# Residual boundaries of a two-block transformer kernel: running sums that end with the sixth tile of eight

## The chip, the cores and the metric

The kernel runs on one core of a Trainium2 chip. Its time is the device time of one launch in microseconds (us). Five engines take part: PE (TensorE, matmuls), DVE (VectorE), ACT (ScalarE), POOL (GpSimd) and SP (SyncE, which issues DMAs here). Each engine works through a queue of its own, in an order that is fixed when the kernel is built; an instruction whose input is not there yet holds up all that stand behind it in the same queue.

## What is computed

x is 256 tokens by 1024 features in fp32. Two layers of a first block (attention, pooling and gated linear attention, beside a second sequence of 256 context tokens that is carried through the first layer only) and then a second block with two residual steps are applied. Every residual step has the form that follows, and the next stage begins with another norm of the new x:

```python
x = x + gate * rmsnorm(out, post_g)                   # out = merged @ w_out, 1024 features
z = (rmsnorm(x, pre_g) * (1 + scale) + shift) @ w_in  # the next stage
```

with `rmsnorm(x, g) = x * rsqrt(mean(x*x) + eps) * g`, the mean taken over the 1024 features of a token.

## The kernel before

x stands in SBUF with the features on the partitions: 8 tiles of 128 features by 256 tokens. A mean over features is thus a sum over 8 tiles and 128 partitions. All matmuls of weights are done three times (`mm3`, L442): each fp32 operand is split into a high part and a low rest (weights by `split`: a ScalarE cast, L425, and a subtraction, L427, by VectorE or GpSimd; activations in `build_h`), and hi*hi, hi*lo and lo*hi are added up. An output tile of a 1024-to-1024 projection is so 24 matmuls of 128x256 (`pwo`); the last projection (`pdn`) has 66 for a tile.

A residual boundary is the stretch between such a projection and the next one. There are five: the context and x between the two layers ("ctx" and "x" below, about 580 to 646 us of the profiled execution), x before the mixer of the second block ("mpre", about 985 to 1020 us), x before its feed-forward part ("fpre", about 1300 to 1336 us), and the last one, which ends in the output ("final").

The kernel computes what the second norm needs without waiting for the new x. With o the gained output, the mean of (x + r\*o)^2 is the mean of x^2, plus r times twice the mean of x\*o, plus r^2 times the mean of o^2. So `collect` takes each of the 8 projection tiles as it comes: ScalarE squares it (L512) and applies the gain to get o (L519; for the last tile VectorE, L517), VectorE multiplies o with x (L523), ScalarE squares o (L524). That gives three terms of 128x256 a tile. Running sums add them up over the tiles: VectorE adds the squares, GpSimd the products and the squares of o (all three L529). When they are complete, TensorE sums them over the partitions with 128x1 matmuls (`token_sums`, L461, into `ps_sa`), two 128-token halves for a term; fp32 makes each of them two records of the trace. VectorE copies the result to `part` (L540, L542).

`boundary` then sums the last tile's terms over the partitions (into `ps_ss`), adds `part` (m, L552), lets GpSimd raise it to the power -1/2 (L488, "the first pow"), spreads r over the partitions by two TensorE transposes (`ps_rb`, L469), sums the other two terms, and makes the new mean A in a chain of five small VectorE instructions (L565 to L569). A second pow and a second pair of transposes follow. `enter` goes through the 8 tiles: `update_x` does x + r\*o, on GpSimd for tiles 0, 1, 3, 5, 7 (L654, L655) and on VectorE for 2, 4, 6 (L657, L658); at the ctx boundary it is GpSimd for 2, 4, 6. `build_h` makes the normed tile (VectorE, L638), its high part (ScalarE, L640 or L643) and its low rest (VectorE, L641 or L644), and the next projection's matmuls (`pen`, `z1_...`; in the trace also `z_misc`) take it.

Where the tile framework's scheduler puts an instruction is decided at build time; `issue_after` asks that GpSimd's updates stand behind the pow.

Of the kernel before, what the change touches and what calls it, by code (L numbers as in the profile page):

```python
# [359 lines left out]
class B:  # L360
# [143 lines left out]
    def collect(self, st, ps, gain, xs, nxt=True):  # L504

        nc, S = self.nc, self.S
        n = ps.shape[-1]
        k = len(st["out"])
        if k == 0:
            st["acc"] = [S.cols(n) for _ in range(3 if nxt else 1)]  # L510
        terms = [S.cols(n) if k else a for a in st["acc"]]
        nc.scalar.activation(terms[0].ap, ps, AF.Square)  # L512
        o_ = S.cols(n)
        for i in range(n // 256):
            c = slice(256 * i, 256 * i + 256)
            if k == 7:
                nc.vector.tensor_scalar(o_.ap[:, c], ps[:, c], gain(k, i), None, ALU.mult)  # L517
            else:
                nc.scalar.mul(o_.ap[:, c], ps[:, c], gain(k, i))  # L519
        if nxt:  # L520
            for i in range(n // 256):
                c = slice(256 * i, 256 * i + 256)
                nc.vector.tensor_mul(terms[1].ap[:, c], o_.ap[:, c], xs[i][k])  # L523
            nc.scalar.activation(terms[2].ap, o_.ap, AF.Square)  # L524
        if k == 7:
            st["last"] = terms
        elif k:
            for e, a, t in zip((nc.vector, nc.gpsimd, nc.gpsimd), st["acc"], terms):
                e.tensor_add(a.ap, a.ap, t.ap)  # L529
            S.drop(*terms)  # L530
        st["out"].append(o_)
        if k == 6:

            m = n // P
            acc = [a.ap for a in st["acc"]]
            p_ = self.pb.tile([P, 512], F32, tag="p", name="ps_sa")
            for i, (a, f) in enumerate(zip(acc, ("mean", "mean2", "mean"))):
                self.token_sums(p_, i * m, a, f=self.c(f))
            st["part"] = self.sm.tile([P, 16], F32, tag="part", name="part")
            nc.vector.tensor_scalar(st["part"][:, :m], p_[:, :m], EPS, None, ALU.add)  # L540
            if nxt:
                nc.vector.tensor_copy(st["part"][:, m:3 * m], p_[:, m:3 * m])  # L542
            S.drop(*st["acc"])

    def boundary(self, st, A, n, nxt=True):

        nc = self.nc
        last, part = [t.ap for t in st["last"]], st["part"]
        ps = self.pa.tile([P, 512], F32, tag="p", name="ps_ss")
        self.token_sums(ps, 0, last[0], f=self.c("mean"))  # L550
        m = self.sm.tile([P, 16], F32, tag="m", name="m")[:, :n]
        nc.vector.tensor_add(m, ps[:, :n], part[:, 0:n])  # L552
        r = self.rsqrt(m, n)
        pr = self.bcast(r, n, self.pa)
        if not nxt:
            self.S.drop(*st["last"])
            return pr, None, None
        ps = self.pb.tile([P, 512], F32, tag="p", name="ps_ss")
        self.token_sums(ps, 0, last[1], f=self.c("mean2"))
        self.token_sums(ps, n, last[2], f=self.c("mean"))  # L560
        self.S.drop(*st["last"])
        t = self.sm.tile([P, 16], F32, tag="bt", name="bt")[:, :n]
        s12 = self.sm.tile([P, 16], F32, tag="bs", name="bs")[:, :2 * n]
        new = self.sm.tile([P, 16], F32, tag="bA", name="bA")[:, :n]
        nc.vector.tensor_add(s12, ps[:, :2 * n], part[:, n:3 * n])  # L565
        nc.vector.tensor_mul(t, r, s12[:, n:2 * n])
        nc.vector.tensor_add(t, t, s12[:, :n])
        nc.vector.tensor_mul(t, t, r)
        nc.vector.tensor_add(new, A, t)  # L569
        pr2 = self.bcast(self.rsqrt(new, n), n, self.pb)  # L570
        return pr, pr2, new

# [75 lines left out]
def update_x(b, k, st, xs, s_, pr, rs, on_pool):  # L648

    nc = b.nc  # L650
    o_ = st["out"][k]
    if on_pool:
        with b.tc.issue_after(b.chain_end.ins):
            nc.gpsimd.tensor_mul(o_.ap, o_.ap, rs.ap)  # L654
            nc.gpsimd.tensor_add(xs[s_][k], xs[s_][k], o_.ap)  # L655
    else:
        nc.vector.tensor_mul(o_.ap, o_.ap, pr[:, 0:256])  # L657
        nc.vector.tensor_add(xs[s_][k], xs[s_][k], o_.ap)  # L658
    b.S.drop(o_)


def enter(b, st, xs, s_, A, h, gain, shift, pool):

    pr, pr2, new = b.boundary(st, A, 2)
    rs = b.S.cols(256)
    b.nc.scalar.copy(rs.ap, pr[:, 0:256])
    for k in range(8):
        update_x(b, k, st, xs, s_, pr, rs, k in pool)
        build_h(b, k, xs, (s_,), gain, shift, pr2, *h(k))
        if k == 7:  # L670
            b.S.drop(rs)
        yield new


def trunk(b, l, xs, st, A):

    nc, S = b.nc, b.S
    full = l == 0
    ALLC, XC = slice(0, 512), slice(256, 512)
# [4 lines left out]
    v = b.vec(f"l{l}")  # L684
# [14 lines left out]
    if st is None:  # L699
        load_x(b, xs)  # L700
        mod_chunk(b, l, 0, True, lambda: first_units((2, 3)))
        ps = b.pa.tile([P, 512], F32, tag="p", name="ps_ss")
        for s_ in range(2):
            acc, t = S.cols(256), S.cols(256)
# [6 lines left out]
        A = b.sm.tile([P, 16], F32, tag="bA", name="bA")[:, :4]  # L711
# [5 lines left out]
    gain_, shift_ = (lambda k, s_: G[:, k, s_:s_ + 1]), (lambda k, s_: shift[:, k, s_:s_ + 1])  # L717
    if st is None:
        h = []
        for k in range(8):  # L720
            if k in MOD_AT:
                mod_chunk(b, l, MOD_AT.index(k) + 1, True)
            h.append((S.get(F32R), S.get(F32R)))
            build_h(b, k, xs, (0, 1), gain_, shift_, pr2, *h[k])
            for w, ps in zip(ws, pss):
                b.mm3(ps, w, h[k:], ALLC, off=k * P, start=k == 0, stop=k == 7)
        S.put(*b.slot[0])
    else:
        h, st = st
        xpart = enter(b, st, xs, 1, A[:, 2:4], lambda k: [t[:, XC] for t in h[k]], gain_, shift_, (0, 1, 3, 5, 7))  # L730
        A = next(xpart)
        for w, ps in zip(ws, pss):
            b.mm3(ps[:, 0:256], w, h, slice(0, 256))
        for k in range(8):
            if k:
                next(xpart)
            for w, ps in zip(ws, pss):
                b.mm3(ps[:, XC], w, h[k:k + 1], XC, off=k * P, start=k == 0, stop=k == 7)
        for _ in xpart:
            pass  # L740
# [523 lines left out]
    for j in range(0, 8, 2):  # L1264
        u = b.unit(("wo", l, j))
        for i in range(2):
            w = b.split(u[:, i * 1024:(i + 1) * 1024], 1024)
            ps = b.pmm.tile([P, 512], F32, tag="p", name="pwo")
# [19 lines left out]
    for w in held:  # L1288
        next(ctx)
        ps = b.pmm.tile([P, 512], F32, tag="p", name="pwo")  # L1290
# [177 lines left out]
def second_block(b, xs, st, A):  # L1468
    nc = b.nc
# [3 lines left out]
    v = b.vec("b2")  # L1473

    def pairs(h):
        return [(a, c) for a, c, _ in h]

    def halves():
        r_ = S.get(F32R)
        return r_[:, 0:256], r_[:, 256:512], r_  # L1480

    def column(w, name):
        ps = b.pmm.tile([P, 512], F32, tag="p", name=name)
        b.mm3(ps[:, C], w, hp, C)
        return ps
# [7 lines left out]
    def enter2(st, g, keys):  # L1493

        h, ws, pss = [], [], []
        for key in keys:
            u = b.unit(key)
            for i in range(2):
                if len(ws) < 3:
                    ws.append(b.split(u[:, i * 1024:(i + 1) * 1024], 1024))  # L1500
                    pss.append(b.pmm.tile([P, 512], F32, tag="p", name="pen"))

        def tile_(k):
            h.append(halves())
            return h[k][0:2]

        for k, new in enumerate(enter(b, st, xs, 1, A, tile_, lambda k, s_: v(g, k), None, (0, 1, 3, 5, 7))):
            for w, ps in zip(ws, pss):
                b.mm3(ps[:, C], w, pairs(h[k:]), C, off=k * P, start=k == 0, stop=k == 7)
        return h, new, pss, u[:, 1024:2048]  # L1510

    h, A, pss, rest = enter2(st, "mpre", [("win2", 14, 15), ("win2", 16, 17)])
    hp = pairs(h)
    cslots = b.unit_slots(("c2",), 3)
# [113 lines left out]
    for ps in (*pss, column(b.split(rest, 1024), "y")):  # L1628
        t = S.cols(256)
# [369 lines left out]
    st = {"out": []}  # L1999
    for j in range(0, 8, 2):  # L2000
        u = b.unit(("wo2", j))
        for i in range(2):
            w = b.split(u[:, i * 1024:(i + 1) * 1024], 1024)
            ps = b.pmm.tile([P, 512], F32, tag="p", name="pwo2")
# [3 lines left out]


    h, A, pss, rest = enter2(st, "fpre", [("up", 0), ("up", 1)])  # L2010
    hp = pairs(h)
    f = []
    nf = FF // P
    for j in range(nf):
# [3 lines left out]
        for i in range(2):  # L2018
            if j < 2 and 2 * j + i < 3:
                ps = pss[2 * j + i]  # L2020
            else:
                ps = column(b.split(rest if j == 1 else u[:, i * 1024:(i + 1) * 1024], 1024), "pup")
# [14 lines left out]
    st = {"out": []}  # L2037
    n = 0
    ps = None
    for un in range(11):  # L2040
        u = b.unit(("down", un))
        for i in range(2):
            hi, lo = b.split(u[:, i * 1024:(i + 1) * 1024], 1024)
            for k8 in range(8):
                k = n % nf
                if k == 0:
                    ps = b.pmm.tile([P, 512], F32, tag="p", name="pdn")
# [5 lines left out]
    pr, _, _ = b.boundary(st, A, 2, nxt=False)  # L2053
    rs = S.cols(256)
    nc.scalar.copy(rs.ap, pr[:, C])
    for k in range(8):
        o_ = st["out"][k]
# [63 lines left out]
```

## Time and profile before

| what | value |
|---|---|
| median of 3 runs | 1535.64 us (1535.45 to 1537.04) |
| the profiled execution's own time | 1536.71 us |
| its span, first to last instruction | 1534.9 us |
| mean granted TensorE clock | 0.96 |
| PE / PEld / DVE / ACT / POOL busy | 93% / 79% / 70% / 46% / 28% |

Rows below give the start (us), the length (us), the engine, the source line, the operation, the tiles, the shapes and, in brackets, the idle time of the engine just before and what ended it. The trace joins like instructions that follow one another: "x4" is four of them. The clock column is a share of TensorE's full 2.4 GHz; 0.5 is its lower level of 1.2 GHz.

### The profile page before, as it was taken

Reading aid. Unit: us, or ns where it says so; the run is one execution under the profiler, and the core shown is the slowest. Engines: PE = TensorE matmul, PEld = TensorE weight load, DVE = VectorE, ACT = ScalarE, POOL = GpSimd, SP = SyncE. Lnnn points to the kernel's source line nnn. Section 1 sums busy time; section 2 is a strip of 40 time slices with the busy share of each in tenths; the row PEclk is TensorE's granted clock in tenths of the full one; section 3 lists DMA queues with packets and bytes.
Section 4 is the critical chain, followed back from the end, with each engine's and each line's share of the span. In section 5 each row is a group of like instructions: output and inputs, shape, how many; then the busy total and the mean of one; then the engine's idle time right before and its main releaser. Section 6 shows DMA issues by size and latency. Waiting matters only on the chain. (4 is left out here: it accounts for less than half of the span.)

```text
span 1534.9 us, 27423 instructions
## 1 busy us (share of the span) xinstructions
PE 1427.4 (93%) x10700; PEld 1212.0 (79%) x10700; DVE 1070.7 (70%) x2113; ACT 713.5 (46%) x1307; POOL 433.8 (28%) x428
## 2 busy tenths in 40 slices
PE   5999999999899999899998899979899999799997
PEld 1676776777788788886877789978668999699997
DVE  4455557877779865755589876758988549698843
ACT  3434445343433764454454445633532435366642
POOL 1010003445341004520035341344644003521212
PEclk8999999999999999999989999978999999799999
DMA  9534440321133363335024335844221325266660
GB/s 358 185 109 141 134 149 17 104 76 56 45 94 117 130 197 99 97 110 165 19 79 124 91 111 172 266 141 125 78 84 37 98 62 169 74 206 181 179 187 32
DMA packets 61041, 187.91 MB, mean 122 GB/s; under 512 B 7024, under 2 KB 8560, under 8 KB 60912
## 3 DMA queue, kind: packets, MB, share of 16 engines
q1 hardware_dynamic: 60912, 186.17, 38.5%
q8 instruction: 84, 1.38, 0.4%
q14 instruction: 45, 0.37, 0.1%
HBM read 180.11 MB, written 6.03 MB: 121 GB/s over the span
## 5 line engine op out<-in xcount | busy, mean ns | idle before, releaser
L425 ACT CAST wh<-raw 128x1024 fp32r<-128x1024 f32 (+1 forms) x296 | 279.4, 949 | 255.9 <-PE y L442 50.6
L427 DVE TENSOR_TENSOR wl<-raw,wh 128x1024 fp32r<-128x1024 f32 (+1 forms) x225 | 263.1, 1170 | 163.9 <-ACT wh L425 160.9
L427 POOL TENSOR_TENSOR wl<-raw,wh 128x1024 fp32r<-128x1024 f32 (+1 forms) x71 | 144.6, 2037 | 641.9 <-ACT wh L425 624.8
L442 PE MATMUL z_merge<-s,wh 128*128 128x512 f32 (+1 forms) x768 | 199.6, 350 | 0.0
L442 PEld LDWEIGHTS z_merge<-s,wh 128*128 128x128 f32 x768 | 135.5, 197 | 17.4 <-issue 1.5
L442 PE MATMUL z_merge<-s,wl 128*128 128x512 f32 (+1 forms) x384 | 133.0, 346 | 0.0
L442 PE MATMUL pbr<-s,wh 128*128 128x256 f32 (+1 forms) x512 | 120.6, 327 | 2.9 <-ACT s L432 2.0
L442 PE MATMUL pup<-s,wh 128*128 128x256 f32 x656 | 118.5, 283 | 0.1
L442 PEld LDWEIGHTS pup<-s,wh 128*128 128x128 f32 x656 | 102.5, 192 | 0.2 <-ACT wh L425 0.2
L442 PE MATMUL y<-s,wh 128*128 128x256 f32 x496 | 99.6, 297 | 0.0
L442 PEld LDWEIGHTS pbr<-s,wh 128*128 128x128 f32 x512 | 86.8, 192 | 12.3 <-ACT s L432 2.6
L442 PE MATMUL pwo<-s,wh 128*128 128x256 f32 (+1 forms) x448 | 91.4, 302 | 2.3 <-ACT s L1251 1.7
L442 PE MATMUL pup<-s,wl 128*128 128x256 f32 x328 | 92.8, 283 | 0.0
L442 PEld LDWEIGHTS y<-s,wh 128*128 128x128 f32 x496 | 79.8, 196 | 7.4 <-issue 4.9
L442 PE MATMUL pbr<-s,wl 128*128 128x256 f32 (+1 forms) x256 | 83.1, 325 | 0.0
L442 PEld LDWEIGHTS z_merge<-s,wl 128*128 128x128 f32 x384 | 75.9, 198 | 8.5 <-issue 0.8
L442 PEld LDWEIGHTS pwo<-s,wh 128*128 128x128 f32 x448 | 73.1, 194 | 5.5 <-ACT s L1251 1.9
L1138 ACT ACTIVATE s<-s 128x512 f32<-128x512 f32 (+1 forms) x64 | 33.3, 524 | 89.1 <-DVE s L1137 77.9
L442 PE MATMUL y<-s,wl 128*128 128x256 f32 x248 | 71.7, 289 | 0.0
L432 ACT CAST s<-s 128x256 fp32r<-128x256 f32 (+1 forms) x88 | 42.6, 487 | 57.1 <-DVE s L1208 14.3
L442 PE MATMUL pwo<-s,wl 128*128 128x256 f32 (+1 forms) x224 | 67.6, 302 | 1.5 <-DVE wl L427 1.5
L442 PE MATMUL pdn<-s,wh 128*128 128x256 f32 x352 | 63.4, 283 | 0.0
(490 smaller groups left out, 3545.7 us busy)
## 6 DMA issues: line engine op xcount, KB each, us to landing
raw<-wts SPq DMA_DIRECT2D x294, 512.0 KB, 4.3
s<-wts SPq DMA_DIRECT2D x57, 256.0 KB, 5.1
s5t<-s SPq DMA_DIRECT2D x16, 256.0 KB, 2.0
s<-s5t SPq DMA_DIRECT2D x16, 256.0 KB, 3.3
s<-xc SPq DMA_DIRECT2D x8, 256.0 KB, 5.3
x<-xc SPq DMA_DIRECT2D x8, 256.0 KB, 5.0
s<-tabs SPq DMA_DIRECT2D x4, 256.0 KB, 3.8
out<-s SPq DMA_DIRECT2D x8, 128.0 KB, 1.8
```

The costliest lines, as they stand in the source:

```text
L425: self.nc.scalar.copy(hi[:, :n], src)
L427: self.last_lo = eng.tensor_sub(lo[:, :n], src, hi[:, :n])
L432: self.nc.scalar.copy(hi, src)
L442: self.nc.tensor.matmul(ps, u, v[:, cols], start=start and n == 0, stop=stop and n == last)
L1138: nc.scalar.activation(E[:, lo:], E[:, lo:], AF.Exp, scale=1.0 / TAU)
```

## The change

The running sums end with tile 5, the sixth; the terms of tiles 6 and 7 both go to the sums over partitions in `boundary`, where TensorE adds the two tiles up in PSUM. GpSimd updates x for tiles 2, 3, 5, 7 and VectorE for 0, 1, 4, 6 at the three boundaries x, mpre and fpre. VectorE's updates are asked to stand behind the last instruction of the small chain.

```diff
-        if k == 7:
-            st["last"] = terms
+        if k > 5:
+            st.setdefault("last", []).append(terms)
         elif k:
             for e, a, t in zip((nc.vector, nc.gpsimd, nc.gpsimd), st["acc"], terms):
                 e.tensor_add(a.ap, a.ap, t.ap)
             S.drop(*terms)
         st["out"].append(o_)
-        if k == 6:
+        if k == 5:
...
-        last, part = [t.ap for t in st["last"]], st["part"]
+        last, part = [[t.ap for t in ts] for ts in zip(*st["last"])], st["part"]
+        last_tiles = [t for ts in st["last"] for t in ts]
...
-        self.token_sums(ps, 0, last[0], f=self.c("mean"))
+        self.token_sums(ps, 0, *last[0], f=self.c("mean"))
...
-        self.token_sums(ps, 0, last[1], f=self.c("mean2"))
-        self.token_sums(ps, n, last[2], f=self.c("mean"))
+        self.token_sums(ps, 0, *last[1], f=self.c("mean2"))
+        self.token_sums(ps, n, *last[2], f=self.c("mean"))
...
-        nc.vector.tensor_add(new, A, t)
+        self.chain_new = nc.vector.tensor_add(new, A, t)
...
     else:
-        nc.vector.tensor_mul(o_.ap, o_.ap, pr[:, 0:256])
-        nc.vector.tensor_add(xs[s_][k], xs[s_][k], o_.ap)
+        with b.tc.issue_after(b.chain_new.ins):
+            nc.vector.tensor_mul(o_.ap, o_.ap, pr[:, 0:256])
+            nc.vector.tensor_add(xs[s_][k], xs[s_][k], o_.ap)
...
-        xpart = enter(b, st, xs, 1, A[:, 2:4], lambda k: [t[:, XC] for t in h[k]], gain_, shift_, (0, 1, 3, 5, 7))
+        xpart = enter(b, st, xs, 1, A[:, 2:4], lambda k: [t[:, XC] for t in h[k]], gain_, shift_, (2, 3, 5, 7))
...
-        for k, new in enumerate(enter(b, st, xs, 1, A, tile_, lambda k, s_: v(g, k), None, (0, 1, 3, 5, 7))):
+        for k, new in enumerate(enter(b, st, xs, 1, A, tile_, lambda k, s_: v(g, k), None, (2, 3, 5, 7))):
```

TensorE's queue at mpre before the change, from the last three of the 24 matmuls of tile 7 on (wh167 and wl167 are the high and low halves of its weights, s28 and s22 activations, s32_668 the running sums of squares and of products, s17_669 those of the squares of o):

```order
L442 MATMUL pwo_9884<-s28_666_9592,wh167_9880 128x256
L442 MATMUL pwo_9884<-s22_667_9593,wh167_9880 128x256
L442 MATMUL pwo_9884<-s28_666_9592,wl167_9881 128x256
L461 MATMUL ps_sa_9870<-cons_89,s32_668_9629 128x1 x4
L461 MATMUL ps_sa_9870<-cons_89,s17_669_9630 128x1 x2
L461 MATMUL ps_ss_9936<-cons_89,s12_676_9863 128x1 x2
L469 MATMUL ps_rb_9943<-cons_89,r_9941 128x128 x2
```

All matmuls of the projection stood ahead of the first one that takes a running sum. The same place after the change (wh166 is tile 6, wh167 tile 7; the running sums are s22_670 and s32_671):

```order
L442 MATMUL pwo_9855<-s28_669_9601,wh166_9851 128x256
L442 MATMUL pwo_9855<-s45_668_9600,wl166_9852 128x256
L442 MATMUL pwo_9888<-s23_654_9572,wh167_9884 128x256
L461 MATMUL ps_sa_9837<-cons_89,s22_670_9637 128x1 x4
L461 MATMUL ps_sa_9837<-cons_89,s32_671_9638 128x1 x2
L442 MATMUL pwo_9888<-s31_655_9573,wh167_9884 128x256
L442 MATMUL pwo_9888<-s23_654_9572,wl167_9885 128x256
L442 MATMUL pwo_9888<-s49_656_9576,wh167_9884 128x256
```

The sums of the running totals now stand one matmul into tile 7, with 23 matmuls of tile 7 behind them. At fpre the sums were likewise behind the whole of tile 7; TensorE's queue there after the change (wh228 and wl228 are tile 6's weights, s21_867 and s3_868 the running sums):

```order
L442 MATMUL pwo2_13489<-s61_863_13226,wh228_13485 128x256 x2
L442 MATMUL pwo2_13489<-s61_863_13226,wl228_13486 128x256
L461 MATMUL ps_sa_13471<-cons_89,s21_867_13271 128x1 x2
L442 MATMUL pwo2_13489<-s34_864_13229,wh228_13485 128x256 x2
L442 MATMUL pwo2_13489<-s34_864_13229,wl228_13486 128x256
L442 MATMUL pwo2_13489<-s53_865_13232,wh228_13485 128x256 x2
L442 MATMUL pwo2_13489<-s53_865_13232,wl228_13486 128x256
L442 MATMUL pwo2_13489<-s26_866_13235,wh228_13485 128x256
L461 MATMUL ps_sa_13471<-cons_89,s21_867_13271 128x1 x2
L461 MATMUL ps_sa_13471<-cons_89,s3_868_13272 128x1 x2
L442 MATMUL pwo2_13489<-s26_866_13235,wh228_13485 128x256
L442 MATMUL pwo2_13489<-s26_866_13235,wl228_13486 128x256
```

They have moved into tile 6, the squares 15 matmuls into it and the others 22, so that 2 matmuls of tile 6 and the 24 of tile 7 stand behind them. VectorE's queue at mpre before the change, from the last running sum to the small chain (bs and bt are its values, s23_673 an o tile that it updates):

```order
L529 TENSOR_TENSOR s32_668_9629<-s32_668_9629,s11_675_9786 128x256
L540 TENSOR_SCALAR part_9877<-ps_sa_9870 128x2
L542 COPY part_9877<-ps_sa_9870 128x4
L517 TENSOR_SCALAR s7_671_9665<-pwo_9884,GP1_1272 128x256
L552 TENSOR_TENSOR m_9939<-ps_ss_9936,part_9877 128x2
L523 TENSOR_TENSOR s11_675_9786<-s7_671_9665,x3_76 128x256
L565 TENSOR_TENSOR bs_9952<-ps_ss_9946,part_9877 128x4
L566 TENSOR_TENSOR bt_9951<-r_9941,bs_9952 128x2
L657 TENSOR_TENSOR s23_673_9708<-s23_673_9708,ps_rb_9943 128x256
L567 TENSOR_TENSOR bt_9951<-bt_9951,bs_9952 128x2
```

Updates of x stood between the instructions of the small chain. The same place after the change (line numbers are one or two higher there):

```order
L529 TENSOR_TENSOR s22_670_9637<-s22_670_9637,s4_677_9794 128x256
L540 TENSOR_SCALAR part_9844<-ps_sa_9837 128x2
L542 COPY part_9844<-ps_sa_9837 128x4
L427 TENSOR_TENSOR wl170_9938<-raw102_0_9933,wh170_9937 128x1024
L523 TENSOR_TENSOR s17_675_9716<-s32_671_9638,x3_76 128x256
L517 TENSOR_SCALAR s40_679_9914<-pwo_9888,GP1_1272 128x256
L553 TENSOR_TENSOR m_9947<-ps_ss_9942,part_9844 128x2
L523 TENSOR_TENSOR s50_678_9913<-s40_679_9914,x3_76 128x256
L566 TENSOR_TENSOR bs_9964<-ps_ss_9954,part_9844 128x4
L567 TENSOR_TENSOR bt_9963<-r_9949,bs_9964 128x2
L568 TENSOR_TENSOR bt_9963<-bt_9963,bs_9964 128x2
L569 TENSOR_TENSOR bt_9963<-bt_9963,r_9949 128x2
```

The first row is now tile 5's sum and no longer tile 6's, the copies to `part` come before a weight subtraction (L427) and both last products, and the small chain is in one piece, with the updates of x behind it.

## Rows read from the trace of the kernel before

**Rows 1.** Page, part 1: busy time, share of the span, instructions.

```profile
PE 1427.4 (93%) x10700; PEld 1212.0 (79%) x10700; DVE 1070.7 (70%) x2113; ACT 713.5 (46%) x1307; POOL 433.8 (28%) x428
```

**Rows 2.** Timeline, TensorE at the ctx and x boundaries.

```profile
605.86 0.61 PE L461 MATMUL ps_sa<-cons,s 128*128 128x1 f32 x4 [1.26 <-DVE s L529]
...
608.37 1.05 PE L461 MATMUL ps_sa<-cons,s 128*128 128x1 f32 x8 [0.97 <-POOL s L529]
...
628.44 0.58 PE L461 MATMUL ps_sa<-cons,s 128*128 128x1 f32 x4 [2.82 <-DVE s L529]
...
634.48 0.58 PE L442 MATMUL z_misc<-s,wl 128*128 128x256 f32 x1 [1.15 <-DVE wl L427]
```

**Rows 3.** Timeline, VectorE and GpSimd at ctx: tile 5's running sums.

```profile
603.11 0.80 DVE L529 TENSOR_TENSOR s<-s,s 128x256 f32<-128x256 f32 x1 [0.47 <-ACT s L512]
...
605.54 0.84 POOL L529 TENSOR_TENSOR s<-s,s 128x256 f32<-128x256 f32 x1 [0.36 <-DVE s L523]
```

**Rows 4.** Timeline, TensorE at mpre.

```profile
999.06 0.28 PE L442 MATMUL pwo<-s,wl 128*128 128x256 f32 x1
...
999.42 0.28 PE L442 MATMUL pwo<-s,wl 128*128 128x256 f32 x1
1001.87 2.18 PE L461 MATMUL ps_sa<-cons,s 128*128 128x1 f32 x12 [2.17 <-DVE s L529]
...
1006.53 1.71 PE L461 MATMUL ps_ss<-cons,s 128*128 128x1 f32 x8
```

**Rows 5.** Timeline, VectorE at mpre.

```profile
998.43 0.41 DVE L529 TENSOR_TENSOR s<-s,s 128x256 f32<-128x256 f32 x1
...
1004.09 0.16 DVE L540 TENSOR_SCALAR part<-ps_sa 128x2 f32<-128x2 f32 x1 [2.37 <-PE ps_sa L461]
...
1008.27 0.16 DVE L565 TENSOR_TENSOR bs<-ps_ss,part 128x4 f32<-128x4 f32 x1 [2.84 <-PE ps_ss L461]
...
1009.76 0.15 DVE L569 TENSOR_TENSOR bA<-bA,bt 128x2 f32<-128x2 f32 x1
...
1013.01 0.48 DVE L638 SCALAR_TENSOR_TENSOR s<-x,vec_b,ps_rb 128x256 f32<-128x256 f32 x1 [1.97 <-POOL x L655]
...
1014.48 2.58 DVE L641 TENSOR_TENSOR s<-s,s 128x256 fp32r<-128x256 f32 x3
```

**Rows 6.** Timeline, GpSimd and ScalarE at mpre.

```profile
998.65 0.79 POOL L529 TENSOR_TENSOR s<-s,s 128x256 f32<-128x256 f32 x1 [0.43 <-DVE s L523]
...
1000.10 1.03 ACT L425 CAST wh<-raw 128x1024 fp32r<-128x1024 f32 x1
...
1002.26 2.34 POOL L427 TENSOR_TENSOR wl<-raw,wh 128x1024 fp32r<-128x1024 f32 x1
1005.18 0.82 POOL L488 TENSOR_TENSOR r<-m,cons 128x2 f32<-128x2 f32 x1 [0.57 <-DVE m L552]
```

**Rows 7.** Windows: PE, PEld, DVE, ACT, POOL busy (x), clock, DMA share, GB/s.

```profile
1000.00:1002.00 2.00, 0.13 (x2) 0.16 (x2) 1.72 (x3) 1.41 (x3) 1.37 (x2) 1.00 0.97 377
1002.00:1004.00 2.00, 2.00 (x13) 2.00 (x13) 0.00 (x0) 0.00 (x0) 2.00 (x2) 0.64 0.79 281
...
1016.00:1018.00 2.00, 2.00 (x11) 2.00 (x11) 2.00 (x5) 0.52 (x2) 1.92 (x3) 0.50 0.00 0
```

**Rows 8.** Timelines at fpre: TensorE, VectorE and GpSimd.

```profile
1309.07 1.29 DVE L529 TENSOR_TENSOR s<-s,s 128x256 f32<-128x256 f32 x2
...
1312.96 0.28 PE L442 MATMUL pwo<-s,wl 128*128 128x256 f32 x1
...
1312.60 3.25 POOL L529 TENSOR_TENSOR s<-s,s 128x256 f32<-128x256 f32 x3
...
1319.38 1.21 DVE L427 TENSOR_TENSOR wl<-raw,wh 128x1024 fp32r<-128x1024 f32 x1
...
1321.13 0.88 POOL L488 TENSOR_TENSOR r<-m,cons 128x2 f32<-128x2 f32 x1 [4.09 <-DVE m L552]
```

**Rows 9.** Source view: GpSimd's additions at fpre, ns min/median/max, first and last start.

```profile
L529 POOL TENSOR_TENSOR s<-s,s x4: 719/871/1706, 1312.6 to 1316.2; 128x256 f32<-128x256 f32 x4
```

More of the change, by code (lines that the diff above doesn't have):

```diff
@@ L555, in boundary @@
         if not nxt:
-            self.S.drop(*st["last"])
+            self.S.drop(*last_tiles)
             return pr, None, None
         ps = self.pb.tile([P, 512], F32, tag="p", name="ps_ss")
-        self.token_sums(ps, 0, last[1], f=self.c("mean2"))
-        self.token_sums(ps, n, last[2], f=self.c("mean"))
-        self.S.drop(*st["last"])
+        self.token_sums(ps, 0, *last[1], f=self.c("mean2"))
+        self.token_sums(ps, n, *last[2], f=self.c("mean"))
+        self.S.drop(*last_tiles)
         t = self.sm.tile([P, 16], F32, tag="bt", name="bt")[:, :n]
```

## The prediction

> **What bounds the kernel now.** I read the busy shares first: TensorE is busy for 93% of the span, the others far less [rows 1]. Time is thus won or lost where TensorE stands idle, or where work is added to its queue. Then I read TensorE's timeline at the boundaries. In brackets each row says how long it stood idle and for whom. It is twice the running sums that it waits for at ctx (1.26 and 0.97 us), once at x (2.82) [rows 2], 2.17 at mpre [rows 4]. So the sums of tile 6 are late today, by 2 to 3 us, and the change takes that tile out of them. Last I read who works in those stretches: VectorE and GpSimd, with weight subtractions (L427, 1.2 to 2.3 us each [rows 6, 8]) in the same queues as the additions.
>
> The second thing to see is the clock. Behind an idle stretch TensorE's granted clock falls: in the window 1000 to 1002 us the engine is busy for 0.13 us, in the next the clock is 0.64 of full and later 0.50, its lower level [rows 7]. At the lower level 2 us hold 11 matmuls, which makes one 0.18 us; at full clock the last matmuls of mpre's tile 7 follow at 0.12 (0.36 for three) [rows 4, 7]. Eight 128x1 records take 1.71 us at the low clock [rows 4] and 1.05 at full clock [rows 2], or about 0.115 each at full clock where they stand in a row (x12 would be 1.4).
>
> **The change, step by step.** What it does to the sums is not only to end them earlier: TensorE's queue takes them earlier. At mpre they move from behind tile 7 to one matmul into it, at fpre into tile 6. Whoever waits there holds up the rest of the projection, so the question is whether tile 5's sums are ready by then.
>
> mpre, the sums. Tile 7's last matmul starts at 999.42, so its first, 23 before, at 996.66, and the second would at 996.78 [rows 4]. Tile 5's squares are added by VectorE at 998.43 + 0.41 = 998.84 [rows 5], its last GpSimd addition ends at 998.65 + 0.79 = 999.44 [rows 6]. TensorE therefore waits 2.1 us with 23 matmuls behind it. Four records (0.46) run up to GpSimd's end, eight (0.92) reach 1000.4, and the 23 matmuls at 0.12 end about 1003.2. With the clock fallen behind the wait they need up to 23 x 0.06 = 1.4 more; I take 1.1, since the clock was full for the first 0.5 us of the window after the idle one [rows 7], and 1004.3. Before, tile 7 ended at 999.70.
>
> mpre, up to the first pow. The last weight unit's cast (1.03) needs tile 7's weight buffer, and GpSimd's subtraction (2.34) stands between it and the pow [rows 6]. That is 3.4, with a hand-over 3.5 us behind tile 7: 1007.8, where the pow stood at 1005.18. This is **+2.6** (+1.5 without the clock). Before, the pow came 5.5 us behind tile 7, since tile 6's sums and the copies at 1004.09 [rows 5] stood between; that gain is in these numbers.
>
> mpre, behind the pow. Six terms more are in the second sums: 14 records against 8 behind the transposes. At the low clock the 6 cost 6 x 0.21 = **+1.3**; at full clock the whole stretch is instead 0.1 shorter than the 1.71 paid now [rows 4]. The small chain loses the updates between its parts: 1008.27 to 1009.91 now [rows 5], **-0.4** (five instructions of 0.15 with their latencies). Tile 0 is no longer behind GpSimd's pow and its four updates: from the chain's end to L638 of tile 0 are 3.10 us (1009.91 to 1013.01 [rows 5]); of it the pow (0.82 [rows 6]), the transposes and hand-overs stay, 1.67 by these rows: **-1.4**. Its low half stands behind tile 2, which still waits for GpSimd: **+0.5**. Together 0.0 at the low clock, -1.4 at full. So mpre is about **+2.6** (from +0.2 to +3.8, the upper end with tile 0's gain lost to its low half).
>
> At fpre it is the same arithmetic. Tile 7's last matmul starts at 1312.96 [rows 8], so tile 6 began 47 before, at 1307.32, and the sums' place, 15 matmuls in, is 1309.12. VectorE's two additions end at 1310.36 [rows 8]: wait 1.2. After 0.2 for two matmuls of sums and 7 of projection, 1311.7. GpSimd's products of tile 5 are the second of three additions from 1312.60 on, so from about 1313.46 [rows 8]; that one took up to 1.71, more than twice the shortest, 0.72 [rows 9], next to VectorE's subtraction. Without that neighbour I take 0.85: ready at 1314.3, wait 2.6. Eight records, then 26 matmuls: 1318.4 at full clock, 1320.1 with the clock fallen; before 1313.24. The pow stood at 1321.13, 7.9 behind tile 7, because VectorE's subtraction (1.21) at 1319.38 and L517 with m (0.54 more, up to 1321.13) came last [rows 8]. These stay, with a cast of 1.1 and hand-overs: 3.1 behind tile 7, 1323.2, **+2.1** (+0.4 without the clock). Behind the pow 0.0 again. fpre: **+2.1** (-1.1 to +3.2).
>
> ctx and x. At ctx the sums move 26 matmuls forward, to 6 and 13 matmuls into tile 6. TensorE was at the first of the two at 605.86 - 1.26 = 604.60 [rows 2], so it now gets there at 604.60 - 3.12 = 601.48 and waits for tile 5's squares until 603.91 [rows 3]: 2.4. The second wait ends with GpSimd at 606.38 [rows 3], 1.13 or so after TensorE gets there. That is 3.6 against 2.23, **+1.4**. The two boundaries add 24 records to a stretch in which TensorE has work all the time: 24 x 0.115 = **+2.8**. In return the waits of 2.82 and 1.15 at x [rows 2] shrink; between nothing and all of 3.97 comes back, and I take half, **-2.0**. Trunk: **+2.2** (0 to +4).
>
> final. Four more records of 0.115, of which half can run before tile 7 is there, and one VectorE sum less: **+0.1**.
>
> Sum: 2.6 + 2.1 + 2.2 + 0.1 = +7.0 on the profiled execution's 1536.71, so 1543.7. That execution lay 1.07 above the median; against the median it is 1542.6, and as two of the terms are at the upper part of their bounds I say 1542.0.
>
> One more cost I looked at. VectorE now has four tiles to update at a boundary instead of three. Its low halves (L641) take 0.86 us each while GpSimd is at work [rows 5], an addition of the same size 0.41 [rows 5] where GpSimd stood idle for its first half, until 998.65 [rows 6]. If such an extra addition and multiplication were on the path, a boundary would cost 0.9 more, +2.7 in all. I put it off the path, because TensorE at its lower clock needs some 2 us for the matmuls of one tile. The Trainium skill, "GPSIMD Engine Reference", section "Specifications", says that GpSimd shares its SBUF interfaces with VectorE, and that VectorE's instructions with two SBUF inputs contend with it. The two durations agree; by that rule the +2.7 would be due if VectorE led, and it speaks against the change.
>
> **The rivals.**
> - *Gains and losses cancel.* The waits at the sums are there, but the clock stays up behind them, or the x boundary gives back nearly all. Then mpre is +0.1 (1.5 - 1.4), fpre -1.0 (0.4 - 1.4), trunk 0 to +2.8: -0.9 to +2, or 1535 to 1538. For it: at x a wait of 2.82 is followed by records of 0.145 [rows 2], so the clock was up at first. Against it: at mpre a wait of 2.17 was followed by 0.64 and 0.50 [rows 4, 7].
> - *The sums are there in time, and it is faster.* Without tile 6, the adders might run earlier, since their queues are shorter in front of them. The deciding point: at mpre tile 5's last addition has to end by 996.78, 2.6 us earlier than now, at fpre 3.8 earlier in all. Then tile 7 ends later by the 12 records alone (1.4): 1001.1 at mpre, the pow 3.5 behind it at 1004.6, -0.6; at fpre 1314.6 and 3.1 behind it 1317.7, -3.4. Without its waits the trunk is -2.23 - 3.97 + 2.8 = -3.4. Together -7.4, or 1528.2. Against it: the tile-5 additions stand behind no tile-6 work today, and their inputs come from tile 5's own squares and products.
> - *VectorE becomes the bound* in building the tiles: +2.7 on top or, with the sums in balance, alone, 1538 to 1545.
> - *The change does nothing here* cannot be: sums move in the queue and the records come on top.
>
> **Chances.** A measurement of this kernel tells about 0.2%, 3.1 us, from no change: 1532.6 to 1538.7. Forecast, the sums hold TensorE up: 0.57, 1539 to 1547. Cancel: 0.26. Faster: 0.12. VectorE: 0.05. The range that holds it 8 times in 10 leaves out the faster rival and what lies beyond both the waits and VectorE: 1535 to 1548. Faster by over 0.2%: 0.12. Within: 0.25. Slower: 0.63.
>
> **What would show it.** Right: TensorE's rows of the sums at mpre carry a wait of about 2 us one matmul into tile 7, at fpre two waits in tile 6; tile 7 ends 3 to 5 us later than before at mpre, 5 to 7 at fpre; the first pow comes about 3.5 behind it; the clock is low in the last matmuls of the projection; the pow-to-first-tile time falls by 1 to 1.5 us. Wrong: no wait at the sums, or tile 7 ending where it did; then the additions came earlier, and the faster rival holds. A clock of 1.00 behind the waits speaks for the second case; a wait of `pen` for L639 or L642 with GpSimd idle for the fourth.

## The result, and the profile after

The changed kernel takes 1547.51 us (median of 8 runs, 1545.63 to 1550.58) against 1537.15 us of the kernel before in as many runs beside it: a ratio of 1.0064, with a 95% interval from 1.0046 to 1.0082. It is 10 us slower. The profiled execution took 1549.95 us (span 1548.2), which is 2.4 above its median.

TensorE has 52 records more, and GpSimd 14 instructions fewer (two running sums of tile 6 at four boundaries, the update of one tile at three; page, part 1, to be read against [rows 1]):

```profile
PE 1442.9 (93%) x10752; PEld 1225.2 (79%) x10752; DVE 1074.4 (69%) x2114; ACT 713.7 (46%) x1307; POOL 422.5 (27%) x414
```

Where the time went can be read from the first and last start of TensorE's tiles, which the tile view gives for every tile. All times are starts in us, the end of the span apart; the last column is the changed kernel's time less that of the kernel before:

| place | before | changed | later by |
|---|---|---|---|
| first `pwo`, ahead of the first boundary | 573.1 | 576.2 | 3.1 |
| last `z_misc`, the end of the x boundary | 658.5 | 666.4 | 7.9 |
| last `z_merge`, ahead of mpre | 972.8 | 979.5 | 6.7 |
| first `pen` of mpre | 1014.0 | 1024.6 | 10.6 |
| last `y`, ahead of fpre | 1274.0 | 1283.5 | 9.5 |
| last `pup`, behind fpre | 1458.8 | 1471.5 | 12.7 |
| last `pdn` | 1522.9 | 1535.6 | 12.7 |
| end of the span | 1534.9 | 1548.2 | 13.3 |

The first 3.1 us lie ahead of anything that was changed; two executions differ by that (in the eleven traces of this case the first `pwo` starts between 571.6 and 577.8). The rest is 3.6 for ctx and x (4.8 at their end, of which 1.2 come back), 2.8 for mpre (3.9 at its first `pen`), 3.2 for fpre and 0.6 for the end: 10.2, about what the medians differ by.

TensorE's timeline at mpre, to be read against [rows 4]:

```profile
1003.31 0.28 PE L442 MATMUL pwo<-s,wh 128*128 128x256 f32 x1
1005.62 2.63 PE L461 MATMUL ps_sa<-cons,s 128*128 128x1 f32 x12 [2.03 <-DVE s L529]
1008.11 0.56 PE L442 MATMUL pwo<-s,wh 128*128 128x256 f32 x1
1008.47 0.41 PE L442 MATMUL pwo<-s,wl 128*128 128x256 f32 x1
1008.68 0.63 PE L442 MATMUL pwo<-s,wh 128*128 128x256 f32 x2
...
1012.75 0.28 PE L442 MATMUL pwo<-s,wl 128*128 128x256 f32 x1
1012.88 0.50 PE L461 MATMUL ps_ss<-cons,s 128*128 128x1 f32 x4
1014.34 0.83 PE L461 MATMUL ps_ss<-cons,s 128*128 128x1 f32 x6 [0.96 <-ACT s L512]
...
1017.80 2.99 PE L461 MATMUL ps_ss<-cons,s 128*128 128x1 f32 x14
...
1024.58 1.01 PE L442 MATMUL pen<-s,wh 128*128 128x256 f32 x3 [1.22 <-ACT s L641]
```

The first matmul of tile 7 starts at 1003.31, then TensorE stands idle for 2.03 us for the running sums, and only at 1012.75 starts the last of the 24: 9.4 us for a tile that took 2.8 before. The windows show the other half of that (columns as in [rows 7]):

```profile
1004.00:1006.00 2.00, 0.38 (x3) 0.41 (x3) 1.47 (x3) 0.95 (x2) 1.58 (x2) 0.92 0.74 175
1006.00:1008.00 2.00, 2.00 (x11) 2.00 (x11) 0.00 (x0) 0.00 (x0) 0.05 (x1) 0.50 0.86 333
...
1010.00:1012.00 2.00, 2.00 (x11) 2.00 (x11) 0.00 (x0) 0.00 (x0) 0.00 (x0) 0.50 0.99 253
1012.00:1014.00 2.00, 1.38 (x11) 1.29 (x10) 0.00 (x0) 1.04 (x2) 0.00 (x0) 0.87 0.68 260
```

Behind the wait the granted clock is at its lower level until past 1012, and nearly all of the held-up tile is computed in that stretch. VectorE, ScalarE and GpSimd do nothing from 1010 to 1012: tile 7 is not there yet.

GpSimd, ScalarE and VectorE at mpre (timelines; [rows 5, 6]):

```profile
1005.28 0.77 POOL L529 TENSOR_TENSOR s<-s,s 128x256 f32<-128x256 f32 x1 [0.42 <-DVE s L523]
1012.96 1.04 ACT L425 CAST wh<-raw 128x1024 fp32r<-128x1024 f32 x1 [3.69 <-DMA raw<-wts]
1014.08 2.34 POOL L427 TENSOR_TENSOR wl<-raw,wh 128x1024 fp32r<-128x1024 f32 x1 [8.03 <-ACT wh L425]
1016.38 0.88 POOL L488 TENSOR_TENSOR r<-m,cons 128x2 f32<-128x2 f32 x1
...
1015.28 1.42 DVE L523 TENSOR_TENSOR s<-s,x 128x256 f32<-128x256 f32 x1
1020.83 0.16 DVE L566 TENSOR_TENSOR bs<-ps_ss,part 128x4 f32<-128x4 f32 x1 [4.12 <-PE ps_ss L461]
...
1021.68 0.16 DVE L570 TENSOR_TENSOR bA<-bA,bt 128x2 f32<-128x2 f32 x1
...
1023.62 0.47 DVE L639 SCALAR_TENSOR_TENSOR s<-x,vec_b,ps_rb 128x256 f32<-128x256 f32 x1
```

The pow starts at 1016.38, 3.5 us behind tile 7's end (taken as 1012.88, where the next records start). GpSimd's subtraction ahead of it waits for ScalarE's cast. The profile puts the cast's own wait down to the transfer of the raw weights; in e5 below the cast starts just as close behind tile 7's last matmul (0.20 us, here 0.21), and there the wait is for the projection. From the chain's end (1021.84) to tile 0's norm are 1.8 us, where it was 3.1. TensorE at fpre ([rows 8]) and at ctx and x ([rows 2]):

```profile
607.03 0.61 PE L461 MATMUL ps_sa<-cons,s 128*128 128x1 f32 x4 [2.21 <-DVE s L529]
609.39 1.58 PE L461 MATMUL ps_sa<-cons,s 128*128 128x1 f32 x8 [0.82 <-POOL s L529]
...
631.45 0.58 PE L461 MATMUL ps_sa<-cons,s 128*128 128x1 f32 x4 [1.33 <-DVE s L529]
...
1319.72 0.61 PE L461 MATMUL ps_sa<-cons,s 128*128 128x1 f32 x4 [0.96 <-DVE s L529]
...
1323.49 1.86 PE L461 MATMUL ps_sa<-cons,s 128*128 128x1 f32 x8 [2.22 <-POOL s L529]
```

### The profile page after: what moved, and what is told of

It reads as the page before. It is cut to its first block, busy times and chain, and to the rows that moved or that the text cites. A ratio compares the mean times of both kernels' runs of the same rounds, so it can differ in the third digit from the quotient of the medians.

```text
span 1548.2 us, 27494 instructions
## 1 busy us (share of the span) xinstructions
PE 1442.9 (93%) x10752; PEld 1225.2 (79%) x10752; DVE 1074.4 (69%) x2114; ACT 713.7 (46%) x1307; POOL 422.5 (27%) x414
## 5 line engine op out<-in xcount | busy, mean ns | idle before, releaser
L427 DVE TENSOR_TENSOR wl<-raw,wh 128x1024 fp32r<-128x1024 f32 (+1 forms) x225 | 262.6, 1168 | 170.3 <-ACT wh L425 167.3
L427 POOL TENSOR_TENSOR wl<-raw,wh 128x1024 fp32r<-128x1024 f32 (+1 forms) x71 | 144.4, 2034 | 657.2 <-ACT wh L425 640.1
L442 PE MATMUL pwo<-s,wh 128*128 128x256 f32 (+1 forms) x448 | 98.6, 316 | 2.3 <-ACT s L1253 1.7
L442 PEld LDWEIGHTS pwo<-s,wh 128*128 128x128 f32 x448 | 78.8, 208 | 5.5 <-ACT s L1253 1.9
```

The costliest lines, as they stand in the source:

```text
L427: self.last_lo = eng.tensor_sub(lo[:, :n], src, hi[:, :n])
L442: self.nc.tensor.matmul(ps, u, v[:, cols], start=start and n == 0, stop=stop and n == last)
```

## The experiments

Theory: the sums of the running totals now stand inside the projection, tile 5's additions are not ready there, and the rest of the projection (with all that waits for tile 7) is held up and then done at the lower clock. Rival 1: the 52 records more cost the time by themselves. Rival 2: VectorE, with four tiles to update, is the new bound. Each kernel was timed in 5 rounds beside the kernel before; a ratio is to that kernel, and 0.1% is 1.5 us.

| kernel | ratio, 95% interval |
|---|---|
| the change | 1.0064 (1.0046 to 1.0082) |
| e1: sums end with tile 5, old share-out of updates | 1.0086 (1.0064 to 1.0108) |
| e2: new share-out of updates alone | 0.9963 (0.9948 to 0.9977) |
| e3: the change, sums behind tile 7 | 0.9959 (0.9944 to 0.9974) |
| e4: before, with the 52 records | 1.0057 (1.0041 to 1.0073) |
| e5: the change, filler at mpre | 1.0045 (1.0029 to 1.0061) |
| e6: e3, second sums ahead of the transposes | 0.9931 (0.9912 to 0.9951) |
| e7: e2, second sums ahead of the transposes | 0.9964 (0.9949 to 0.9978) |
| e8: the change, sums behind tile 7 at ctx and x only | 1.0034 (1.0021 to 1.0047) |
| e9: e6, weight split behind the first pow | 0.9941 (0.9920 to 0.9962) |

**e1, the sums alone.** The change without its second half; the lists of GpSimd's tiles are (0, 1, 3, 5, 7) again:

```diff
-        with b.tc.issue_after(b.chain_new.ins):
-            nc.vector.tensor_mul(o_.ap, o_.ap, pr[:, 0:256])
-            nc.vector.tensor_add(xs[s_][k], xs[s_][k], o_.ap)
+        nc.vector.tensor_mul(o_.ap, o_.ap, pr[:, 0:256])
+        nc.vector.tensor_add(xs[s_][k], xs[s_][k], o_.ap)
...
```

> The running sums end with tile 5 as in the change; GpSimd keeps tiles 0, 1, 3, 5, 7 and VectorE's updates may stand between the small chain's instructions, as before. The theory that the place of the sums in TensorE's queue holds up the projection expects the same waits as in the changed kernel (about 2.0 us at mpre, 1.0 and 2.2 at fpre, 2.2 and 0.8 at ctx) and a time above the changed kernel's by what the new share-out of updates gives, 1 to 1.4 us at each of three boundaries: 3 us over it, +13 on the kernel before. The rival that VectorE's four tiles are what costs time expects less than the changed kernel, +6 to +8.

Measured 1.0086, or +13 us: what the theory gave. The wait at mpre is 2.03 us, as in the changed kernel. So the share-out of the updates is not what costs; by the ratios it gives some 3 us back, though the two intervals overlap.

**e2, the updates alone.** The kernel before with the lists (2, 3, 5, 7) and with VectorE's updates behind the small chain.

> The running sums end with tile 6 as before; only the share-out of the updates (GpSimd 2, 3, 5, 7) and their place behind the small chain are changed. The theory of the held-up projection expects a gain of 1 to 1.4 us at each of x, mpre and fpre: -3 to -4 us on the kernel before, with 0.4 less for the small chain and about 1.7 instead of 3.1 us from its end to tile 0's norm. The rival that VectorE becomes the bound expects +2 to +3.

Measured 0.9963, 5.7 us faster (3.5 to 8.0 by the interval): the right sign, and more than the 3 to 4 expected, though the interval holds these too. VectorE's timeline of e2 at mpre:

```profile
1009.77 0.16 DVE L569 TENSOR_TENSOR bA<-bA,bt 128x2 f32<-128x2 f32 x1
1009.85 0.74 DVE L658 TENSOR_TENSOR s<-s,ps_rb 128x256 f32<-128x256 f32 x2
1010.51 1.28 DVE L659 TENSOR_TENSOR x<-x,s 128x256 f32<-128x256 f32 x2
1011.71 0.86 DVE L638 SCALAR_TENSOR_TENSOR s<-x,vec_b,ps_rb 128x256 f32<-128x256 f32 x2
```

From the chain's end at 1009.93 to tile 0's norm are 1.78 us instead of 3.10, since x of tiles 0 and 1 is updated while GpSimd does the second pow. Rival 2 falls.

**e3, the sums behind tile 7.** The changed kernel, with one thing moved: the sums are emitted when tile 7 is collected, and stand behind its last matmul.

```diff
-        if k == 5:
+        if k == 7:
...
-            for i, (a, f) in enumerate(zip(acc, ("mean", "mean2", "mean"))):
-                self.token_sums(p_, i * m, a, f=self.c(f))
+            with self.tc.issue_after(self.last_mm.ins):
+                for i, (a, f) in enumerate(zip(acc, ("mean", "mean2", "mean"))):
+                    self.token_sums(p_, i * m, a, f=self.c(f))
```

> The changed kernel, but the sums of the running totals stand behind the last matmul of tile 7 in TensorE's queue, at every boundary. Nothing else is undone: the 52 records more are there, and tile 6 is still out of the running sums. The theory of the held-up projection expects tile 7 to end where it did before (no wait in the projection) and the first pow 2 to 4 us earlier than in the kernel before at mpre and fpre: in all -3 to -8 us on the kernel before, some 15 below the changed kernel. The rival that the records themselves cost most expects it to stay above the kernel before by 4 or more.

Measured 0.9959, which is 6.3 us below the kernel before and 16 us below the changed one, with all its records. TensorE at mpre in e3:

```profile
1002.04 1.40 PE L461 MATMUL ps_sa<-cons,s 128*128 128x1 f32 x12
1003.30 1.47 PE L461 MATMUL ps_ss<-cons,s 128*128 128x1 f32 x10
1006.92 0.69 PE L469 MATMUL ps_rb<-cons,r 128*128 128x128 f32 x2 [2.16 <-POOL r L488]
1007.40 2.98 PE L461 MATMUL ps_ss<-cons,s 128*128 128x1 f32 x14
```

At mpre no wait stands at the sums: when the projection is through, tile 5's additions are done, and the twelve records follow one another at 0.105 (1002.04 to 1003.30). At fpre one is left, but no matmul of the projection stands behind it:

```profile
1314.05 1.05 PE L461 MATMUL ps_sa<-cons,s 128*128 128x1 f32 x8 [1.47 <-POOL s L529]
```

From the start of tile 7's last matmul to the pow are 4.1 us at mpre and 5.1 at fpre, where it was 5.8 and 8.2: 1.7 and 3.1 earlier, with 2 to 4 expected. This settles that the place of the sums is what the change lost by. But the 14 second records now cost 2.98 us on the way from the first pow to the small chain, against 1.71 before. Compared with e2, which has no tile 6 out of the sums and no more records, e3 is the same within the intervals: at mpre, what the earlier pow gives, the records behind it mostly take.

**e4, the records alone.** The kernel before; every sum of the last tile also adds a tile of zeros.

```diff
-        self.token_sums(ps, 0, last[0], f=self.c("mean"))
+        self.token_sums(ps, 0, last[0], Z, f=self.c("mean"))
...
```

> The kernel before with the same number of records more (52): the last tile's three sums each add up a second tile of zeros, which changes no value. The running sums, their place and the updates stay. The theory of the held-up projection expects what the records cost by themselves: 24 in the trunk at 0.115 to 0.2 us (2.8 to 4), six behind the transposes at mpre and fpre at 0.21 (1.3 each), half a microsecond at the end, and little for the sums of the squares, which stand beside casts: +4 to +7 us. The rival that they are the whole of it expects +10.

Measured 1.0057, +8.8 us: above the theory's 4 to 7 (the interval is 6.3 to 11.2), near the rival's 10. Two rows of TensorE's timeline of e4, the first at ctx and the second at mpre, show why:

```profile
612.11 0.56 PE L461 MATMUL ps_ss<-cons,zero 128*128 128x1 f32 x2
...
1011.61 0.57 PE L461 MATMUL ps_ss<-cons,zero 128*128 128x1 f32 x2
```

Their records follow one another at 0.21 us (612.11, 612.54, 612.97), at mpre as at ctx: here all but the last four, at the end, stand where the clock is down. 24 in the trunk (ctx and x) are then 5.1, not 2.8. The low stretch grows with them, too: in the windows from 600 to 660 us the clock falls short of 1.00 by 12.0 us in sum, against 5.1 in the kernel before. So e4 prices the records together with a longer low stretch. Records and place are thus not two shares of one sum: in e4, where TensorE waits at every boundary as before, they cost nearly what the whole change costs; in e3 the rows show of them 1.3 us for the second sums at each later boundary and some 2 at ctx and at x (14 in 2.99 and 3.15 us, against 8 in 0.95), and the kernel is faster than before. Rival 1 is half right: the records are dear, but they alone don't say whether the kernel is slower.

**e5, the clock by itself.** The changed kernel with eight matmuls of 128x128 that nothing reads, in the place of the wait at mpre. The sums keep their place, one matmul into tile 7.

```diff
+            for _ in range(8 if mm else 0):
+                last = self.nc.tensor.matmul(p_[:, 256:384], self.ident, self.ident, start=True, stop=True)
...
```

> The changed kernel, with eight matmuls of 128x128 f32 that nothing reads put in front of the running totals' sums at mpre alone, one matmul into tile 7, where TensorE otherwise waits. The sums stay at their place and their inputs come no earlier. If the clock is what the wait costs beside itself, the clock stays up, the 23 matmuls and 12 records behind the sums take 2.8 + 1.4 us instead of the 4.6 + 2.5 measured, and the first pow comes 2 to 3 us earlier against the start of tile 7; the whole time falls by 2 to 3 us below the changed kernel. If the clock has nothing to do with the wait, or falls anyway, tile 7 ends where it does in the changed kernel or later, and the time is the same or up to 1 us more.

Measured 1.0045. That is 2.9 us below the changed kernel, but the two intervals overlap, so the time alone does not show a gain. The traces show one: from the last `z_merge` to the first `pen` of mpre are 42.1 us instead of the changed kernel's 45.1, and to the last `y` 300.8 instead of 304.0. TensorE and ScalarE at mpre, then the windows:

```profile
998.85 0.28 PE L445 MATMUL pwo<-s,wh 128*128 128x256 f32 x1
998.97 1.94 PE L554 MATMUL ps_sa<-cons 128*128 128x128 f32 x16
1001.07 1.64 PE L468 MATMUL ps_sa<-cons,s 128*128 128x1 f32 x12 [0.16 <-DVE s L537]
...
1005.28 0.28 PE L445 MATMUL pwo<-s,wl 128*128 128x256 f32 x1
...
1005.48 1.04 ACT L426 CAST wh<-raw 128x1024 fp32r<-128x1024 f32 x1 [3.12 <-PE pwo L445]
```

```profile
1002.00:1004.00 2.00, 2.00 (x19) 2.00 (x19) 1.15 (x4) 0.36 (x1) 0.00 (x0) 1.00 0.75 256
1004.00:1006.00 2.00, 1.90 (x18) 1.82 (x16) 0.00 (x0) 0.52 (x1) 0.00 (x0) 1.00 0.90 314
```

The inputs come no earlier and the sums start as late (2.2 us behind tile 7's first matmul, 2.3 in the changed kernel). Yet the clock stays at 1.00, and from tile 7's first matmul to its last are 6.4 us instead of 9.4. At mpre the wait itself costs 2.0 us, the clock behind it another 3.0.

**e6 and e7, the second sums ahead of the transposes.** In e3 and in e2 the second sums are emitted before the first transposes, so that they run while TensorE waits for the pow.

```diff
-        pr = self.bcast(r, n, self.pa)
...
         self.token_sums(ps, n, *last[2], f=self.c("mean"))
+        with self.tc.issue_after(self.last_sum.ins):
+            pr = self.bcast(r, n, self.pa)
```

> The kernel with the sums behind tile 7 (e3), and the second sums (14 records) moved ahead of the first transposes in TensorE's queue, where it waits for the first pow. The theory that records cost time only where they stand behind the pow expects about 2 us at mpre and fpre less than e3, since 2.99 us of records then lie beside 1.6 to 2.2 us of waiting: -4 on e3, -9 to -11 on the kernel before. The rival that the pow's wait is not free, because the terms of the last tile come late, expects e3's time within 1 us.

> The kernel before with the new share-out of updates (e2) and its 8 second records moved ahead of the first transposes; the running sums end with tile 6 as before, no records added. By the same theory about 1 to 1.2 us at mpre and fpre less than e2 (the wait for the pow there is 1.15 and 2.0 us, the records 1.71): -2 on e2, -7 to -8 on the kernel before. The rival expects e2's time.

e6 measured 0.9931, the lowest ratio of all (with e9 inside its interval) and 10.6 us below the kernel before; e7 0.9964, no different from e2. In the traces both win the same locally: from the start of `ps_sa` to the first `pen` at fpre 13.2 us in e3 and 12.3 in e6, 11.4 in e2 and 10.4 in e7. TensorE in e6 at mpre shows why it is 0.9 and not 2:

```profile
1005.90 3.15 PE L461 MATMUL ps_ss<-cons,s 128*128 128x1 f32 x14 [1.33 <-DVE s L523]
1008.91 0.67 PE L469 MATMUL ps_rb<-cons,r 128*128 128x128 f32 x2
```

The records start late, because the product of tile 7 (L523) is late: it takes 1.17 us beside GpSimd's weight subtraction. So the second rival holds for half. Gains of 1 us at two places are at the limit of what such a timing resolves; that e6 gained 4 on e3 by the ratios, whose intervals overlap, and e7 nothing on e2, is not explained by them.

**e8, the trunk alone.** e3's move at ctx and x only.

```diff
-        if k == 5:
+        if k == (7 if st["nb"] < 2 else 5):
...
```

> The changed kernel with the sums behind tile 7 at ctx and x alone; at mpre and fpre they stay inside the projection. It tells the share of the trunk from that of the two later boundaries. e3 lay 15 below the changed kernel with all boundaries so changed; from the traces' offsets I expect 5 to 6 of it here (the waits of 2.2, 0.8 and 1.3 us and the clock behind them), so +4 to +6 on the kernel before. If the trunk's loss came from the 24 records and not from their place, it stays within 1 us of the changed kernel.

Measured 1.0034: 4.6 us below the changed kernel, a little less than the 5 to 6 expected, with the wait at mpre (2.00) still there. From the first `pwo` to the last `z_misc` are 85.0 us in its trace, 90.2 in the changed kernel's. Some 5 us of the loss through the place are the trunk's, the rest (1.0034 to 0.9959, 11.5 us) that of mpre, fpre and the end.

**e9, the weights' split behind the pow.** In e6, ScalarE's cast and the subtraction of the weights that follow the first three stand ahead of the pow. Here they are issued behind tile 7's last square, m and the first pow.

```diff
+    with b.tc.issue_after(b.sq.ins), b.tc.issue_after(b.m_ins.ins), b.tc.issue_after(b.pow1.ins):
+        w_rest = b.split(rest, 1024, True)
...
```

> The kernel with the sums behind tile 7 and the second sums ahead of the transposes (e6), and the split of the weights that the next stage needs only behind its first three (cast by ScalarE, subtraction) moved behind the first pow, at mpre and fpre; the subtraction is GpSimd's at both, between its two pows. By the theory that this split is what sets the first pow after tile 7 (3.5 us in the prediction's sum), the pow at mpre comes 1 to 1.8 us earlier against tile 7's end, that at fpre 1.2 to 2, and the chain behind it as much: -2 to -4 on e6, -12 to -15 on the kernel before. The rival, that the second sums' records then set the chain, expects e6's time within 1 us.

Measured 0.9941: no faster than e6. GpSimd and VectorE at mpre, and TensorE at fpre:

```profile
1002.37 0.82 POOL L488 TENSOR_TENSOR r<-m,cons 128x2 f32<-128x2 f32 x1 [2.89 <-DVE m L554]
1003.17 2.34 POOL L427 TENSOR_TENSOR wl<-raw,wh 128x1024 fp32r<-128x1024 f32 x1
...
1002.21 0.41 DVE L523 TENSOR_TENSOR s<-s,x 128x256 f32<-128x256 f32 x1
...
1313.13 2.27 PE L461 MATMUL ps_ss<-cons,s 128*128 128x1 f32 x10
```

At mpre the pow comes 2.8 us behind the start of the twelve records (999.58), and the product takes 0.41 again. At fpre nothing was won: the ten records ahead of m now run at the low clock (2.27 us against 1.38 in e6), and the pow starts 5.5 us behind `ps_sa`, where it was 5.0. What was won at mpre doesn't show at the last `y` (1271.2 against 1271.6 in e6). That TensorE waits for VectorE between mpre and fpre in both (4.9 us in one piece, for the tile `hb`) may be why; that was not tried.

## Why the prediction was right, and where its sizes were off

The sign and the cause came out. The size came out only just: 1542.0 was said, 6.4 us above its base, and 1547.5 measured, 10.4 above the kernel before timed beside it. That is at the upper edge of the range (1535 to 1548) and just above the 1539 to 1547 given to this mechanism. Errors of opposite sign lie in it: the clock cost 3.2 us more than said at mpre and fpre together, the stretches behind the pow 1.3 less. Step by step:

- *The waits.* Said 2.1 at mpre, 1.2 and 2.6 at fpre, 2.4 and 1.13 at ctx; measured 2.03, 0.96 and 2.22, 2.21 and 0.82. Reading the end of tile 5's additions from [rows 3, 5, 6, 8] and the sums' new place from the queue was enough for this; e3 shows that the place is the cause.
- *The clock.* This is the term that was mis-sized. For mpre I took 1.1 us, on the ground that the clock stayed full for a while behind an idle stretch [rows 7]. It fell right at the start of the sums, and the twelve records (2.5 us, said 1.4) and nearly all of the 23 matmuls ran at the lower level: 3.0 us by e5. The price of a matmul there was read too low as well: 0.18 us, from 11 in 2 us [rows 7], counts also matmuls that only reach into the window; by their starts (1008.47, 1008.68 above) they follow at 0.21. Tile 7 took 9.6 us from its first matmul to its end where 7.6 was said. At fpre, where 1.7 were taken, it was 3.0 (eight records in 1.72 us instead of 0.92, 26 matmuls in 5.28 instead of 3.12), with shorter waits: from tile 6's start (1316.81) to tile 7's end (1330.49) 13.7 us, 7.9 more than before, said 6.9. No run tests the clock alone at fpre; its share there is read from the rows. (The prediction's 0.2 us for the first sums at fpre is a slip: they are four records, 0.47 in the trace, and its next time, 1311.7, counts them so.)
- *Up to the pow.* 3.5 us behind tile 7 at mpre, said 3.5; 2.9 at fpre, said 3.1.
- *Behind the pow.* Said 0.0; measured -0.6 and -0.7 (pow to first `pen` 8.2 instead of 8.8 and 8.9). The records' +1.3 (2.99 against 1.71) and the chain's and tile 0's gains (-0.6 and -1.3) came about as said (-0.4 and -1.4). The +0.5 for tile 0's low half did not: the matmul that takes it follows the first `pen` by 1.4 us in e2 and in the kernel before alike.
- *Sums by boundary.* mpre said +2.6, measured 3.9 at its end and 2.8 further on; fpre +2.1, measured 2.1 at its first `pen` and 3.2 at the last `pup`; the end +0.1, measured 0.6.
- *The trunk.* Said +2.2 (0 to 4), measured 4.8 at its end and 3.6 further on. The waits at the sums and the records came about as priced: ctx +0.8 (1.4 said), x gives 1.6 back (2.0), the added records are at full clock. The waits for the pow grew by 0.4. The clock was left out here altogether. In the windows of 10 us from 600 to 660 its shortfall from 1.00 adds up to 5.1 us before and 6.8 in the changed kernel, so 1.7 more; the largest increase is in the window of ctx (before first, changed kernel second):

```profile
610.00:620.00 10.00, 9.52 (x69) 9.32 (x68) 5.19 (x17) 3.37 (x7) 4.18 (x6) 0.83 0.10 28
```

```profile
610.00:620.00 10.00, 9.85 (x58) 9.64 (x58) 1.63 (x6) 1.97 (x5) 0.70 (x1) 0.67 0.11 26
```

  That the waits at the sums bring the clock down in the trunk is not shown, though. In e3 TensorE waits for no running sum at ctx, and the clock falls there all the same, behind 22 records of 128x1 among the matmuls (windows of e3):

```profile
610.00:612.00 2.00, 2.00 (x20) 2.00 (x20) 0.62 (x3) 0.42 (x1) 0.00 (x0) 1.00 0.38 82
612.00:614.00 2.00, 1.80 (x13) 1.59 (x12) 0.49 (x2) 0.07 (x1) 0.82 (x1) 0.72 0.14 49
614.00:616.00 2.00, 2.00 (x11) 2.00 (x11) 0.00 (x0) 0.30 (x1) 0.00 (x0) 0.50 0.00 0
```

  Its shortfall from 600 to 660 is 8.5 us, more than the changed kernel's 6.8. Still the first `pwo` to the last `z_misc` take 84.9 us in e3 against 90.2, and TensorE's waits between them shrink from 6.6 to 1.05. By these sums the place costs the trunk its waits; that it costs it clock as well is not shown.

- *The rule on the shared interfaces.* The Trainium skill, "GPSIMD Engine Reference", section "Specifications", spoke against the change. That the two engines contend, the traces bear out: the product L523 takes 0.41 with GpSimd idle or at its pow (e9) and 1.42 beside GpSimd's subtraction. But VectorE's fourth tile is not on the path: e2 is faster, not slower by 2.7.

## What to carry to other kernels

On an engine with a fixed queue, "sum earlier" also means "wait earlier": read from the built order what stands behind the moved instruction, and from the trace when its inputs are there; a sum that is not needed until the projection is through belongs behind it (e3). Price a wait of TensorE with the clock behind it, which at mpre cost more than the wait (3.0 against 2.0 us), and can be kept up by work that nobody reads (e5). A change in two halves should be timed in halves: the updates' new order was worth 5.7 us, and the sums took 16 away that their place alone gave back; with the second sums ahead of the transposes (e6) the kernel is 0.7% faster than before.

## What the runs showed of the hardware that I had not expected

With eight unused f32 matmuls of 128x128 in the 2 us of the wait at mpre (16 records, 1.94 us) the clock stayed at 1.00 through the whole of the next 4 us; without them it was at 0.50 from the first record behind the wait. But a wait was not always what stood ahead of the fall: in e3 at ctx it came with TensorE idle for 0.20 us at most, behind 22 records of 128x1. The Trainium skill, "TensorE: Matmul & The Clock Gate", section "What's actually happening", names two clock levels of 1.2 and 2.4 GHz. The records agree: 128x1 records follow one another at 0.21 us at the lower level (e4) and at 0.105 at full clock (e3). And work that came off the path ahead of the pow did not always bring the pow forward: in e9 at fpre the ten records in front of it were done at the lower clock, 2.27 us instead of 1.38.
